# The convolution's LayerNorm chain in a two-layer encoder kernel: a raised priority, buffers of its own, one PSUM bank

## The chip, the cores and the metric

The kernel runs on one core of one Trainium2 chip. The metric is the device time of one execution in microseconds (us), the median of several runs. A profiled execution, taken apart from these runs, gives the trace: the instructions of PE (TensorE matmuls; PEld is its weight load), DVE (VectorE), ACT (ScalarE), POOL (GpSimd) and the queue of SP (SyncE), which issues most DMAs.

## The reference

Two layers work on x, 512 tokens of 1024 features in float32. Each adds half a SwiGLU feed-forward network, then a mixer, then half a second feed-forward network, and ends in an RMS norm. The mixer projects the normed x once and has two parts: attention with 8 heads, and a convolution module. The change lies in the convolution's LayerNorm:

```python
def layer_norm(x, g, b):
    mu = jnp.mean(xf, axis=-1, keepdims=True)
    xc = xf - mu
    y = xc * lax.rsqrt(jnp.mean(xc * xc, axis=-1, keepdims=True) + EPS)
    return (y * g + b)

def conv_group(u_raw, conv_w, conv_b, ln_g, ln_b):
    a, g = u_raw[..., :CONV_W], u_raw[..., CONV_W:]
    u = a * jax.nn.sigmoid(g)
    y = lax.conv_general_dilated(u, conv_w, ...)      # causal, depthwise, 31 taps
    return jax.nn.silu(layer_norm(y + conv_b, ln_g, ln_b))

x = x + jnp.concatenate([attn, conv], axis=-1) @ w_out[l]
```

## The kernel before

**Layout.** Features lie on the 128 partitions and tokens along the free axis, so a 512-wide convolution output is four tiles `ys[0..3]` of 128 x 512. A sum over features is a sum over partitions; the kernel makes it on PE with a matrix of ones. A float32 product is made of three PE products of high and low parts (`mm3`, L157 to L160: high x high, high x low, low x high). `split` (L163) makes the parts: ACT casts the high one (L165), DVE subtracts for the low one (L166).

**The order of the work.** The program names tiles and dependences; a planner lays the instructions of each engine in one order when the program is built, by priority (the order in which the lines are traced, unless it is changed) and by when it holds inputs and buffers to be free. On the chip each engine takes its instructions in that order and waits at the first one that isn't ready. `tc.issue_after(i)` places what is traced under it behind instruction i on its engine. `tmp()` (L98) hands out one of 5 temporaries, `bank()` (L101) one of 7 PSUM banks; the eighth PSUM bank, tag `cv`, holds the accumulator of convolution tiles 0 and 3.

**The mixer.** After the projections (L816), a loop over steps (L929) runs the eight heads in stages: `turn` (L833), `scores` (L846, with the maximum on DVE L861 and Exp on ACT L865), `turn_p` (L870, transposes L880 and copies L883), `values` (L886, L895 to L905), and `turn_out` (L908), which splits the output of each pair of heads into `at[0..3]`. The convolution's taps are traced after it (L941): for tiles 0 and 3 on DVE (L953) with ACT's copy out of PSUM at the end (L961), for tile 1 on ACT (L957) and POOL (L959), for tile 2 on PE (L659), ACT and POOL. They fill engines beside attention.

**The chain after the taps (L973 to L998)**, the place of the change:

- `early_groups` (L967): the output projection's first four blocks begin with their attention half, k = 0 to 3, twelve products each, behind the last head's scores. They are placed by hand in four parts: the first ahead of the chain, the second after the mean (L982), the third after the token factor (L988), the fourth after the spread (L990).
- the mean: POOL adds tiles 0, 1 and 2 into a temporary (L975, L976), DVE adds tile 3 (L977), PE spreads the mean over all partitions (L979) into a bank.
- ACT's table for Silu is loaded early by a one-element Silu (L981).
- DVE subtracts the mean from each tile (L985). ACT squares each (L188 into a ring slot, L191 into temporaries), DVE adds the squares (L195).
- `token` (L207): eight one-column matmuls sum the squares (L202), DVE scales (L209), POOL raises to -1/2 (L177).
- `spread` (L214): DVE makes a diagonal in a temporary (L217), PE multiplies it by ones (L221), so that 1/rms stands on all partitions in a bank.
- DVE multiplies each tile by it into a temporary z (L995), ACT applies gain, bias and Silu into another (L997), and `split` makes `cv`.

Then the projection's first four blocks get their convolution half (L1004, k = 4 to 7), and after them blocks 4 to 7 all eight k. Their weights take the buffers that the first four release; POOL makes their low parts (L148). x is updated at L1010, and the second feed-forward network follows.

Of the kernel before, what the change touches and what calls it, by code (L numbers as in the profile page):

```python
# [7 lines left out]
FP = mybir.dt.float32  # L8
# [3 lines left out]
AF = mybir.ActivationFunctionType  # L12
ALU = mybir.AluOpType
AX = mybir.AxisListType

P = 128
D = 1024
S = 512
# [3 lines left out]
H = 8  # L22
# [6 lines left out]
CW = 512  # L29
CK = 31  # L30
F = 2816
NF = F // P
EPS = 1e-6
# [16 lines left out]
QFOLD = 0  # L50
# [1 line left out]
EARLY = "s"  # L52
PRELOAD = 1
E1 = 1
E2 = 2
E3 = 3
WOG = 4
WAKE = 10
KS = (0, 2, 4, 6, 1, 3, 5, 7)
WOP = 4  # L60
# [18 lines left out]
def encoder_kernel(ctx: ExitStack, tc: tile.TileContext, xT, consts, vecs, rgain, wgu1, wd1, wdq1,  # L79
# [8 lines left out]
    psum = ctx.enter_context(tc.tile_pool(name="psum", bufs=7, space=PSUM))  # L88
    uid = [0]

    def nm(s):
        uid[0] += 1
        return f"{s}{uid[0]}"

    def slot(dt=FP, w=S):
        return ring.tile([P, w], dt, tag="r", name=nm("r"))

    def tmp(w=S, dt=FP):  # L98
        return tmps.tile([P, w], dt, tag="t", name=nm("t"))

    def bank():  # L101
        return psum.tile([P, S], FP, tag="ps", name=nm("ps"))

    def tiny(tag, w, dt=FP):
        return small.tile([P, w], dt, tag=tag, name=nm(tag))

    V, A, G, T = nc.vector, nc.scalar, nc.gpsimd, nc.tensor
# [17 lines left out]
    onesm = cpool.tile([P, P], FP, name="onesm")  # L125
# [8 lines left out]
    def vv(l, name):  # L134
        o, w = VOFF[name]
        return vec[:, l, o:o + w]
# [42 lines left out]
    class Stats:  # L179
# [2 lines left out]
        def __init__(self):  # L182
            self.acc = self.tail = None

        def add(self, src, scale=1.0, last=False, eng=None, apart=False):
            if self.acc is None:
                self.acc = slot()
                A.activation(self.acc, src, AF.Square, scale=scale)  # L188
                return
            sq = tmp()  # L190
            A.activation(sq, src, AF.Square, scale=scale)  # L191
            if apart:
                self.tail = sq
                return
            (eng or (V if last else G)).tensor_tensor(self.acc, self.acc, sq, ALU.add)  # L195

        def sums(self):
            ps = bank()
            parts = [self.acc] + ([self.tail] if self.tail is not None else [])
            for part in parts:  # L200
                for t in range(NT):
                    order["sums"] = T.matmul(ps[:, t:t + 1], part[:, t * P:(t + 1) * P], ones[:, 0:1],  # L202
                                             start=part is self.acc and (t == 0 or len(parts) == 1),
                                             stop=part is parts[-1], skip_group_check=len(parts) > 1).ins
            return ps[:, 0:NT]

        def token(self, n):  # L207
            self.ve = small.tile([P, NT], FP, tag="vtok", name=nm("vtok"), bufs=4)
            V.tensor_scalar(self.ve, self.sums(), 1.0 / n, EPS, ALU.mult, ALU.add)  # L209
            r = small.tile([P, NT], FP, tag="rtok", name=nm("rtok"), bufs=4)  # L210
            rsqrt(r, self.ve)
            return r

    def spread(r):  # L214

        dg = tmp()
        V.tensor_tensor(dg.rearrange("p (t j) -> p t j", t=NT),  # L217
                        ident[:, None, :].to_broadcast([P, NT, P]),
                        r[:, :, None].to_broadcast([P, NT, P]), ALU.mult)
        ps = bank()  # L220
        order["spread"] = T.matmul(ps, ones, dg, start=True, stop=True).ins  # L221
        return ps

# [397 lines left out]
    def mix_body(kpool, l, gx, norm, done):  # L621
        u, order = [], {}
        diag = kpool.tile([P, PT, Q], FP, tag="m", name=nm("m"), bufs=11)
# [6 lines left out]
        ys = [kpool.tile([P, S], FP, tag=f"y{c}", name=nm("y"), bufs=1) if n else None for c, n in enumerate(TAPS)]  # L630
# [40 lines left out]
        cqT, ckT, pq, scqs, vs = [], [], [], [], []  # L671
# [159 lines left out]
        heads = [{} for _ in range(H)]  # L831
# [14 lines left out]
        def scores(h):  # L846
            qT, kT = heads[h]["qk"]
            b01, b2, b3 = bank(), bank(), bank()
            if h % 2 == 0:
                heads[h]["sums"] = small.tile([P, NT, 2], FP, tag="sums", name=nm("sums"), bufs=3)  # L850
            sums = heads[h - h % 2]["sums"]
            mx = small.tile([P, NT], FP, tag="mx", name=nm("mx"), bufs=3)
            pi = []
            ps = [slot() for _ in range(3)]
            ps = [ps[0][:, 0:128], ps[0][:, 128:384], ps[1][:, 0:384], ps[2]]
            for i in range(NT):
                n = (i + 1) * P
                o = (b01[:, 0:128], b01[:, 128:384], b2[:, 0:384], b3)[i]
                T.matmul(o, qT[0:DQ, i * P:(i + 1) * P], kT[0:DQ, 0:n], start=True, stop=False)  # L859
                heads[h]["s"] = T.matmul(o[:, n - 64:n], mrow, mneg, start=False, stop=True).ins  # L860
                V.tensor_reduce(mx[:, i:i + 1], o, axis=AX.X, op=ALU.max, negate=True)  # L861
                p = ps[i]
                if QFOLD:
                    V.tensor_tensor(mx[:, i:i + 1], mx[:, i:i + 1], scqs[i][:, h:h + 1], ALU.mult)
                A.activation(p, o, AF.Exp, bias=mx[:, i:i + 1], scale=scqs[i][:, h:h + 1] if QFOLD else 1.0,  # L865
                             accum_out=sums[:, i, h % 2:h % 2 + 1])
                pi.append(p)
            heads[h]["p"] = pi

# [51 lines left out]
        with tc.issue_after(order["turned"]):  # L921
            for t in range(NT):
                ps = up_kv(wv, t)
# [5 lines left out]
        for step in range(H + 6):  # L929
            if step == PSTEP:  # L930
                conv_pe()
            for stage, lag in STAGES:
                h = step - lag
# [6 lines left out]
        cw, cb = vv(l, "cw"), vv(l, "cb")  # L940
        for c, n in enumerate(TAPS):  # L941
            tap = lambda k: cw[:, c * CK + k:c * CK + k + 1]
            acc = psum.tile([P, S], FP, tag="cv", name=nm("cv"), bufs=1) if n < CK else None
            if n and c != PC:
                A.activation(ys[c], u[c], AF.Identity, scale=tap(CK - 1), bias=cb[:, c:c + 1])
            for s in range(n, CK):
                k = CK - 1 - s
                if s == 0:
                    A.activation(acc, u[c], AF.Identity, scale=tap(k), bias=cb[:, c:c + 1])  # L949
                elif s == n:  # L950
                    A.activation(acc[:, s:], u[c][:, :S - s], AF.Copy, scale=tap(k))
                else:
                    V.scalar_tensor_tensor(acc[:, s:], u[c][:, :S - s], tap(k), acc[:, s:], ALU.mult, ALU.add)  # L953
            for s in range(PT if c == PC else 1, n):
                k = CK - 1 - s
                pr = kpool.tile([P, S], FP, tag="pr", name=nm("pr"), bufs=4)
                A.activation(pr[:, s:], u[c][:, :S - s], AF.Copy, scale=tap(k))  # L957
                with tc.issue_after(order["keys"]) if s >= PAUSE or c > 1 else nullcontext():
                    order["conv"] = G.tensor_tensor(ys[c][:, s:], ys[c][:, s:], pr[:, s:], ALU.add).ins  # L959
            if not n:  # L960
                A.copy(u[c], acc)  # L961
                ys[c] = u[c]
            elif n < CK:
                V.tensor_tensor(ys[c][:, n:], ys[c][:, n:], acc[:, n:], ALU.add)
        early = []

        def early_groups(ms):  # L967
            with tc.issue_after(heads[H - 1][EARLY]):
                for m in ms:
                    early.append(bank())  # L970
                    group(early[m], wo[m], at, range(4), KD)

        early_groups(range(E1))  # L973
        ysum = tmp()
        G.tensor_tensor(ysum, ys[0], ys[1], ALU.add)  # L975
        G.tensor_tensor(ysum, ysum, ys[2], ALU.add)  # L976
        V.tensor_tensor(ysum, ysum, ys[3], ALU.add)  # L977
        pm = bank()
        T.matmul(pm, onesm, ysum, start=True, stop=True)  # L979
        if PRELOAD:  # L980
            A.activation(tiny("pre", 1), ysum[:, 0:1], AF.Silu)  # L981
        early_groups(range(E1, E2))  # L982
        st = Stats()
        for c in range(4):
            V.tensor_tensor(ys[c], ys[c], pm, ALU.subtract)  # L985
            st.add(ys[c], eng=V)
        r = st.token(CW)
        early_groups(range(E2, E3))  # L988
        pr = spread(r)
        early_groups(range(E3, WOG))  # L990
        lg, lb = vv(l, "lg"), vv(l, "lb")
        cv = []
        for c in range(4):
            z = tmp()
            V.tensor_tensor(z, ys[c], pr, ALU.mult)  # L995
            s = tmp()
            A.activation(s, z, AF.Silu, bias=lb[:, c:c + 1], scale=lg[:, c:c + 1])  # L997
            cv.append(split(s))  # L998

        ac = at + cv  # L1000
        for m0 in range(0, KD, WOG):
            ms = range(m0, min(m0 + WOG, KD))
            os = [bank() for _ in ms] if m0 else early
# [78 lines left out]
    st = Stats()  # L1082
# [192 lines left out]
```

## Time and profile before

| | us |
|---|---|
| median of 3 runs (lowest to highest) | 1806.21 (1804.67 to 1807.08) |
| the profiled execution's own time | 1806.27 |
| its span, first to last instruction | 1804.5 |
| PE busy | 1785.5 |
| DVE busy | 1497.7 |
| ACT busy | 1095.8 |
| POOL busy | 382.7 |

Read it from PE, which is busy in nearly all of the span. An instruction of PE is counted with a modelled end, so consecutive products overlap in the rows; the distance from one start to the next is what one costs. The mean granted clock of PE is 0.998 of full speed. Feed-forward networks take most of the time; the two mixers are the places where POOL works, and layer 0's convolution norm lies at about 497 to 525 us, layer 1's 894 us later.

### The profile page before, as it was taken

To read this page: it belongs to the slowest core of one execution; us is meant where nothing else is said; L and a number is where in the kernel's file an instruction comes from. 1 tells how busy PE (TensorE), PEld (TensorE's weight loads), DVE (VectorE), ACT (ScalarE), POOL (GpSimd) and SP (SyncE) were. 2 spreads that over 40 slices of the span, in tenths; PEclk is the share of its full clock that TensorE was granted. 3 is DMA by queue.
4 is the path that set the end of the run, shared out by engine and by line. 5 is a ranking of instruction groups with operands and counts; after the bars stand their busy time and mean duration, and the time that the engine had idled before them with its cause. 6 is when DMAs were issued, how large, how long until landed. Compare 5 with 4: busy or idle time off the path is not lost.

```text
span 1804.5 us, 29201 instructions
## 1 busy us (share of the span) xinstructions
PE 1785.5 (99%) x11302; PEld 1584.6 (88%) x11302; DVE 1497.7 (83%) x2309; ACT 1095.8 (61%) x1699; POOL 382.7 (21%) x313
## 2 busy tenths in 40 slices
PE   9999999999999999999999999999999999999998
PEld 7899999888668899999888999998976688999997
DVE  7898988689945989898779989876998559989883
ACT  5675756467843575756645757554777435757564
POOL 1000000258623000000310000002685310000002
PEclk9999999999999999999999999999999999999999
DMA  5657574325103466665426575743260126575742
GB/s 170 164 137 187 128 187 111 107 88 135 53 14 110 122 160 158 158 159 134 123 65 169 124 193 123 193 109 115 75 170 7 36 87 158 144 177 139 181 118 73
DMA packets 71946, 228.26 MB, mean 126 GB/s; under 512 B 8448, under 2 KB 9600, under 8 KB 71808
## 3 DMA queue, kind: packets, MB, share of 16 engines
q1 hardware_dynamic: 55536, 171.87, 30.0%
q0 software_dynamic: 16128, 54.53, 17.6%
q8 instruction: 88, 1.44, 0.3%
q14 instruction: 50, 0.41, 0.1%
q10 hardware_dynamic: 144, 0.00, 0.0%
HBM read 222.19 MB, written 2.10 MB: 124 GB/s over the span
## 4 chain that ended last, share of the span: by engine, by line
PE 56%; DVE 3%; ACT 1%; POOL 0%; issue 0%; ACTq 0%; DVEq 0%; POOLq 0%
PE ps L158 14%; PE ps L160 14%; PE ps L159 14%; PE ps L377 7%; PE ps L378 4%; DVE cv L953 1%; PE ps L902 0%; PE ps L859 0%; DVE mx L861 0%; DVE wl L250 0%; PE ps L202 0%; POOL sck L177 0%; PE ps L880 0%; PE ps L221 0%; DVE kn L810 0%
## 5 line engine op out<-in xcount | busy, mean ns | idle before, releaser
L158 PE MATMUL ps<-r,wh 128*128 128x256 f32 (+1 forms) x2556 | 810.7, 321 | 4.1 <-ACT r L165 1.4
L159 PE MATMUL ps<-r,wh 128*128 128x256 f32 (+1 forms) x2556 | 813.7, 319 | 0.5 <-DVE r L166 0.5
L160 PE MATMUL ps<-r,wl 128*128 128x256 f32 (+1 forms) x2364 | 756.3, 322 | 0.2 <-DVE wl L250 0.2
L158 PEld LDWEIGHTS ps<-r,wh 128*128 128x128 f32 x2556 | 484.1, 189 | 50.5 <-ACT wh L142 3.6
L159 PEld LDWEIGHTS ps<-r,wh 128*128 128x128 f32 x2556 | 485.0, 190 | 37.4 <-DVE r L166 2.6
L160 PEld LDWEIGHTS ps<-r,wl 128*128 128x128 f32 x2364 | 448.6, 190 | 34.8 <-DVE wl L148 0.7
L377 PE MATMUL ps<-xj,wh 128*128 128x512 f32 x864 | 303.8, 391 | 0.0
L142 ACT CAST wh<-raw 128x1024 fp32r<-128x1024 f32 (+3 forms) x148 | 132.4, 901 | 209.6 <-PE ps L159 126.5
L248 ACT CAST wh<-fr 128x1024 fp32r<-128x1024 f32 (+1 forms) x160 | 157.7, 986 | 106.2 <-DVE fr L414 42.3
L394 POOL DMA_DIRECT2D ls<-in_wgu x72 | 62.7, 870 | 734.7 <-ACT ls L393 524.4
L148 DVE TENSOR_TENSOR wl<-raw,wh 128x1024 fp32r<-128x1024 f32 (+3 forms) x132 | 144.6, 1103 | 88.0 <-ACT wh L142 87.4
L250 DVE TENSOR_TENSOR wl<-fr,wh 128x1024 fp32r<-128x1024 f32 (+1 forms) x160 | 182.1, 1138 | 20.5 <-ACT wh L248 20.4
L377 PEld LDWEIGHTS ps<-xj,wh 128*128 128x128 f32 x864 | 161.4, 188 | 30.1
L378 PE MATMUL ps<-xj,ls 128*128 128x256 f32 x576 | 161.3, 280 | 0.0
L959 POOL TENSOR_TENSOR y<-y,pr 128x495 f32<-128x495 f32 (+29 forms) x90 | 120.8, 1343 | 46.6 <-ACT pr L957 41.0
L248 ACT CAST wh<-raw 128x1024 fp32r<-128x1024 f32 (+1 forms) x100 | 98.2, 982 | 45.4 <-PE ps L159 24.6
L250 DVE TENSOR_TENSOR wl<-raw,wh 128x1024 fp32r<-128x1024 f32 (+1 forms) x100 | 113.4, 1134 | 14.2 <-ACT wh L248 13.8
L378 PEld LDWEIGHTS ps<-xj,ls 128*128 128x128 f32 x576 | 108.3, 188 | 0.0
L393 ACT ACTIVATE ls<-fr 128x1024 fp32r<-128x1024 f32 (+1 forms) x56 | 56.1, 1002 | 75.0 <-PE ps L378 42.8
L195 POOL TENSOR_TENSOR r<-r,t 128x512 f32<-128x512 f32 x45 | 74.1, 1656 | 128.8 <-ACT t L191 128.2
L953 DVE SCALAR_TENSOR_TENSOR cv<-m,vec,cv 128x511 f32<-128x511 f32 (+14 forms) x120 | 87.8, 732 | 3.7 <-ACT cv L949 2.2
L394 POOL DMA_DIRECT2D ls<-in_wdq x32 | 27.7, 865 | 262.2 <-ACT ls L393 262.2
(245 smaller groups left out, 2930.8 us busy)
## 6 DMA issues: line engine op xcount, KB each, us to landing
fr<-in_wgu SPq DMA_DIRECT2D x112, 512.0 KB, 4.2
ls<-in_wgu POOLq DMA_DIRECT2D x72, 512.0 KB, 6.3
raw<-in_wgu SPq DMA_DIRECT2D x62, 512.0 KB, 4.5
fr<-in_wdq SPq DMA_DIRECT2D x48, 384.0 KB, 4.7
ls<-in_wdq POOLq DMA_DIRECT2D x32, 384.0 KB, 4.7
raw<-in_wd SPq DMA_DIRECT2D x32, 384.0 KB, 3.1
raw<-in_wd SPq DMA_DIRECT2D x32, 256.0 KB, 2.7
raw<-in_wcv SPq DMA_DIRECT2D x16, 512.0 KB, 3.5
```

What stands on the lines that cost most here:

```text
L142: order["cast"] = A.copy(hi[:, :w], raw[:, :w]).ins
L148: (G if kind in POOLW.split() else V).tensor_tensor(lo[:, :w], raw[:, :w], hi[:, :w].bitcast(FP), ALU.subtract)
L158: T.matmul(o, lh, rh, start=first, stop=False, skip_group_check=free)
L159: T.matmul(o, lh, rl, start=False, stop=False, skip_group_check=free)
L160: order["mm"] = T.matmul(o, ll, rh, start=False, stop=last, skip_group_check=free).ins
L248: A.copy(hi[:, :w], src[:, :w])
L250: order["lo"] = V.tensor_tensor(lo[:, :w], src[:, :w], hi[:, :w].bitcast(FP), ALU.subtract).ins
L377: T.matmul(o, w[0][:, c], both, start=start and k == 0, stop=False, skip_group_check=True)
L378: last = T.matmul(o[:, 0:HS], w[1][:, c], both[:, 0:HS], start=False, stop=k == 3, skip_group_check=True).ins
L394: G.dma_start(out=lo[:, :n], in_=w, accum_op=ALU.add)
L953: V.scalar_tensor_tensor(acc[:, s:], u[c][:, :S - s], tap(k), acc[:, s:], ALU.mult, ALU.add)
L959: order["conv"] = G.tensor_tensor(ys[c][:, s:], ys[c][:, s:], pr[:, s:], ALU.add).ins
```

## The change

The links from the sum of the four tiles to the spread of 1/rms are traced under a raised priority (400 places). Their buffers are tiles that the convolution has done with: the sum, the second and fourth square and the diagonal lie in `u[1]`, the first square, into which the others are added, in `u[2]`, the third in `diag`. The three matmul steps write to the bank with tag `cv`. The early groups 1 to 3 are traced together after the chain. z and the Silu's output are written in place into the tiles `ys`. The table's preload and the Silus are placed behind the last head's Exps, which `scores` now notes.

```diff
-E2 = 2
-E3 = 3
 WOG = 4
+CHAIN = 400
...
+    def behind(ins):
+        stack = ExitStack()
+        for i in ins:
+            stack.enter_context(tc.issue_after(i))
+        return stack
+
+    def conv_bank():
+        return psum.tile([P, S], FP, tag="cv", name=nm("cv"), bufs=1)
...
-        def add(self, src, scale=1.0, last=False, eng=None, apart=False):
+        def add(self, src, scale=1.0, last=False, eng=None, apart=False, into=None):
             if self.acc is None:
-                self.acc = slot()
+                self.acc = slot() if into is None else into
                 A.activation(self.acc, src, AF.Square, scale=scale)
                 return
-            sq = tmp()
+            sq = tmp() if into is None else into
...
-    def spread(r):
+    def spread(r, made=bank, dg=None):
-        dg = tmp()
+        dg = tmp() if dg is None else dg
...
-        ps = bank()
+        ps = made()
...
         early_groups(range(E1))
-        ysum = tmp()
-        G.tensor_tensor(ysum, ys[0], ys[1], ALU.add)
-        G.tensor_tensor(ysum, ysum, ys[2], ALU.add)
-        V.tensor_tensor(ysum, ysum, ys[3], ALU.add)
-        pm = bank()
-        T.matmul(pm, onesm, ysum, start=True, stop=True)
+        st = Stats()
+        with tc.high_priority(CHAIN):
+            ysum = u[1]
+            G.tensor_tensor(ysum, ys[0], ys[1], ALU.add)
+            G.tensor_tensor(ysum, ysum, ys[2], ALU.add)
+            V.tensor_tensor(ysum, ysum, ys[3], ALU.add)
+            pm = conv_bank()
+            T.matmul(pm, onesm, ysum, start=True, stop=True)
+            for c in range(4):
+                V.tensor_tensor(ys[c], ys[c], pm, ALU.subtract)
+                st.add(ys[c], eng=V, into=(u[2], u[1], diag.rearrange("p a b -> p (a b)"), u[1])[c])
+            r = st.token(CW, conv_bank)
+            pr = spread(r, conv_bank, u[1])
         if PRELOAD:
-            A.activation(tiny("pre", 1), ysum[:, 0:1], AF.Silu)
-        early_groups(range(E1, E2))
-        st = Stats()
-        for c in range(4):
-            V.tensor_tensor(ys[c], ys[c], pm, ALU.subtract)
-            st.add(ys[c], eng=V)
-        r = st.token(CW)
-        early_groups(range(E2, E3))
-        pr = spread(r)
-        early_groups(range(E3, WOG))
+            with behind(heads[H - 1]["exps"]):
+                A.activation(tiny("pre", 1), ysum[:, 0:1], AF.Silu)
+        early_groups(range(E1, WOG))
...
-            z = tmp()
-            V.tensor_tensor(z, ys[c], pr, ALU.mult)
-            s = tmp()
-            A.activation(s, z, AF.Silu, bias=lb[:, c:c + 1], scale=lg[:, c:c + 1])
+            z = s = ys[c]
+            V.tensor_tensor(z, z, pr, ALU.mult)
+            with behind(heads[H - 1]["exps"]):
+                A.activation(s, z, AF.Silu, bias=lb[:, c:c + 1], scale=lg[:, c:c + 1])
```

More of the change, by code (lines that the diff above doesn't have):

```diff
@@ L195, in add, with sums @@
             (eng or (V if last else G)).tensor_tensor(self.acc, self.acc, sq, ALU.add)
-        def sums(self):
-            ps = bank()
+        def sums(self, made=bank):
+            ps = made()
             parts = [self.acc] + ([self.tail] if self.tail is not None else [])
@@ L205, in sums, with token @@
             return ps[:, 0:NT]
-        def token(self, n):
+        def token(self, n, made=bank):
             self.ve = small.tile([P, NT], FP, tag="vtok", name=nm("vtok"), bufs=4)
-            V.tensor_scalar(self.ve, self.sums(), 1.0 / n, EPS, ALU.mult, ALU.add)
+            V.tensor_scalar(self.ve, self.sums(made), 1.0 / n, EPS, ALU.mult, ALU.add)
             r = small.tile([P, NT], FP, tag="rtok", name=nm("rtok"), bufs=4)
@@ L219, in spread @@
                         r[:, :, None].to_broadcast([P, NT, P]), ALU.mult)
-        ps = bank()
+        ps = made()
         order["spread"] = T.matmul(ps, ones, dg, start=True, stop=True).ins
@@ L864, in scores @@
                     V.tensor_tensor(mx[:, i:i + 1], mx[:, i:i + 1], scqs[i][:, h:h + 1], ALU.mult)
-                A.activation(p, o, AF.Exp, bias=mx[:, i:i + 1], scale=scqs[i][:, h:h + 1] if QFOLD else 1.0,
-                             accum_out=sums[:, i, h % 2:h % 2 + 1])
+                heads[h].setdefault("exps", []).append(A.activation(p, o, AF.Exp, bias=mx[:, i:i + 1], scale=scqs[i][:, h:h + 1] if QFOLD else 1.0,
+                             accum_out=sums[:, i, h % 2:h % 2 + 1]).ins)
                 pi.append(p)
@@ L942, in mix_body @@
             tap = lambda k: cw[:, c * CK + k:c * CK + k + 1]
-            acc = psum.tile([P, S], FP, tag="cv", name=nm("cv"), bufs=1) if n < CK else None
+            acc = conv_bank() if n < CK else None
             if n and c != PC:
```

## The prediction

> **What bounds the kernel now.** I read the page first, then the engines' busy time in stretches around the end of the mixer, then PE's waits, and last the timeline there, engine by engine.
>
> ```profile
> span 1804.5 us, 29201 instructions
> PE 1785.5 (99%) x11302; PEld 1584.6 (88%) x11302; DVE 1497.7 (83%) x2309; ACT 1095.8 (61%) x1699; POOL 382.7 (21%) x313
> ```
>
> PE is busy for 99% of the span, so only three things can change the time: PE idling, PE at a lower clock, or PE doing other work. The edit leaves PE's products as they are. So the question is what PE loses near the changed lines. The stretch view of layer 0 shows it (columns: stretch, its length, busy time and count of each engine, then the granted clock), with the slow stretch of layer 1 last:
>
> ```profile
> 485.00:495.00 10.00, 10.00 (x72) 6.38 (x71) 9.85 (x20) 6.24 (x19) 0.00 (x0) 1.00 0.01 2
> 495.00:502.70 7.70, 7.70 (x73) 5.22 (x71) 4.95 (x11) 4.68 (x11) 2.54 (x2) 1.00 0.01 2
> 502.70:510.00 7.30, 6.47 (x28) 3.68 (x28) 1.98 (x3) 2.10 (x3) 0.00 (x0) 1.00 0.00 0
> 513.50:516.70 3.20, 1.10 (x8) 1.13 (x9) 1.74 (x3) 0.48 (x1) 0.00 (x0) 0.92 0.00 0
> 516.70:519.50 2.80, 2.80 (x8) 2.22 (x9) 0.85 (x2) 0.00 (x0) 1.03 (x1) 0.50 0.00 0
> 525.00:535.00 10.00, 10.00 (x45) 8.23 (x46) 3.77 (x6) 4.18 (x7) 0.29 (x1) 1.00 0.01 2
> ...
> 1410.60:1413.60 3.00, 3.00 (x8) 2.33 (x9) 0.85 (x2) 0.00 (x0) 1.03 (x1) 0.50 0.00 0
> ```
>
> PE is dense up to 502.7 us and again from 525. Between them it idles, most of all from 513.5 to 516.7, and then runs at half its clock for 2.8 us. DVE paces the stretch to 495 (9.85 of 10.00) and has room after it: 2.75 us free to 502.7, 5.32 us to 510. The timeline of that place, rows of all engines in order of start (start, length, engine, line, what, idle before it and who ended it):
>
> ```profile
> 493.32 0.59 ACT L961 COPY m<-cv 128x512 f32<-128x512 f32 x1 [0.17 <-DVE cv L953]
> 497.16 1.28 POOL L975 TENSOR_TENSOR t<-m,y 128x512 f32<-128x512 f32 x1 [15.60 <-DVE r L166]
> 498.52 1.27 POOL L976 TENSOR_TENSOR t<-t,y 128x512 f32<-128x512 f32 x1
> 506.83 0.69 DVE L905 TENSOR_TENSOR t<-ps,t 128x512 f32<-128x512 f32 x1 [4.22 <-PE ps L902]
> 508.19 1.28 ACT L981 ACT_TABLE_LOAD   x1
> 508.20 0.69 DVE L166 TENSOR_TENSOR r<-t,r 128x512 fp32r<-128x512 f32 x1 [0.68 <-ACT r L165]
> 508.23 0.50 PE L158 MATMUL ps<-r,wh 128*128 128x512 f32 x1 [0.61 <-ACT r L165]
> 508.81 0.68 DVE L977 TENSOR_TENSOR t<-t,m 128x512 f32<-128x512 f32 x1
> 508.95 0.50 PE L159 MATMUL ps<-r,wh 128*128 128x512 f32 x1 [0.22 <-DVE r L166]
> 509.64 1.10 PE L979 MATMUL ps<-t,onesm 128*128 128x512 f32 x2
> 510.78 0.69 DVE L985 TENSOR_TENSOR m<-m,ps 128x512 f32<-128x512 f32 x1 [1.28 <-PE ps L979]
> 513.17 2.28 DVE L195 TENSOR_TENSOR r<-r,t 128x512 f32<-128x512 f32 x3
> 515.60 1.29 PE L202 MATMUL ps<-ones,r 128*128 128x1 f32 x8 [2.10 <-DVE r L195]
> 516.93 0.16 DVE L209 TENSOR_SCALAR vtok<-ps 128x4 f32<-128x4 f32 x1 [1.47 <-PE ps L202]
> 517.17 1.03 POOL L177 TENSOR_TENSOR rtok<-vtok,minus_half 128x4 f32<-128x4 f32 x1 [17.38 <-DVE vtok L209]
> 518.24 0.69 DVE L217 TENSOR_TENSOR t<-cst,rtok 128x512 f32<-128x512 f32 x1 [1.15 <-POOL rtok L177]
> 520.91 1.02 PE L221 MATMUL ps<-t,ones 128*128 128x512 f32 x2
> 521.97 0.69 DVE L995 TENSOR_TENSOR t<-m,ps 128x512 f32<-128x512 f32 x1 [3.04 <-PE ps L221]
> ```
>
> The chain of the convolution's norm runs from L977 at 508.81 to the first use of the spread at 521.97: 13.16 us, in which PE meets it three times (L979, L202, L221). It starts late for two reasons that the rows show: POOL's first add sat 15.60 us because its temporary was still read by L166, and L977, whose inputs were there at 498.52 + 1.27 = 499.79, stood on DVE behind attention's L905 (idle 4.22 us) and L166.
>
> **The change, part by part.** *Buffers of its own* end the 15.60 us: the two adds can go as soon as POOL is done with the taps. *The priority* lets L977 go as soon as its last input, L961's copy, is there at 493.32 + 0.59 = 493.91. So the chain can begin some 15 us earlier and, at its 13.2 us, end near 507. PE's own work then sets the end. What goes from PE's time, in both layers:
>
> ```profile
> PE ps L202 <- DVE r L195: 4.2, 2, 2.1
> ...
> 516.75 0.77 PE L158 MATMUL ps<-m,wh 128*128 128x512 f32 x1
> 519.76 0.40 PE L159 MATMUL ps<-r,wh 128*128 128x512 f32 x1
> 520.00 0.39 PE L160 MATMUL ps<-r,wl 128*128 128x512 f32 x1
> 1410.46 0.76 PE L158 MATMUL ps<-m,wh 128*128 128x512 f32 x1
> 1413.96 0.39 PE L160 MATMUL ps<-r,wl 128*128 128x512 f32 x1
> 524.30 0.39 PE L160 MATMUL ps<-r,wl 128*128 128x512 f32 x1
> 524.83 1.20 PE L158 MATMUL ps<-r,wh 128*128 128x512 f32 x4
> ```
>
> - A, the wait at the squares' sums (from the waits: total, times, longest): 4.2 us.
> - B, the half clock after it. At full clock products start 0.23 us apart (519.76 to 520.00, and the bulk of the stage). In layer 0 seven products took 519.76 - 516.75 = 3.01 us for 7 x 0.23 = 1.61: 1.40 lost. In layer 1 eight took 3.50 for 1.84: 1.66 lost. Together 3.1 us.
> - C, the wait of the first early group for the last head's split: 0.61 + 0.22 = 0.83 us in layer 0, taken twice 1.7 us. It goes if the other three groups, no longer placed by hand behind links of the chain, fill it: k = 0 and 1 of four groups are 24 products, 5.5 us.
>
> A + B + C = 9.0 us. PE is dense behind this place (10.00 of 10.00 from 525), so what is won here is kept.
>
> What it costs. *POOL's add beside a DVE that sets the pace*: it moves from 498.52, where DVE had room, to the end of the taps.
>
> ```profile
> 475.17 6.39 POOL L959 TENSOR_TENSOR y<-y,pr 128x486 f32<-128x486 f32 x5
> 482.05 0.68 DVE L166 TENSOR_TENSOR m<-t,m 128x512 fp32r<-128x512 f32 x1
> ...
> 1438.42 2.85 POOL L148 TENSOR_TENSOR wl<-raw,wh 128x1024 fp32r<-128x1024 f32 x1
> 1439.53 2.82 DVE L148 TENSOR_TENSOR wl<-raw,wh 128x1024 fp32r<-128x1024 f32 x1
> 1448.01 1.23 DVE L148 TENSOR_TENSOR wl<-raw,wh 128x1024 fp32r<-128x1024 f32 x1 [0.22 <-ACT wh L142]
> ```
>
> POOL ends the taps at 481.56; L976 would run to about 482.84. DVE's L166, with two operands in SBUF, starts at 482.05. The pair at 1438 shows what happens: DVE's subtraction, 1.23 us by itself, took 2.82 beside POOL's, ending 1.1 us after POOL's end. So L166 waits 482.84 - 482.05 = 0.8 us, 1.6 us for two layers, in a stretch where DVE paces attention. Bounds: nothing, if L976 falls elsewhere or PE covers it, and 1.27 each, a whole add. I take 0.8. [...]
>
> *The chain in front of attention on DVE.* Its DVE work is 0.68 (L977), 2.39 (L985, 510.78 to 513.17), 2.28, 0.16 and 0.69: 6.2 us, out of 2.75 + 5.32 us free to 510, where L977 is counted as busy already. Attention's last split may come some 3 us later than 508.89. That is covered: it feeds only k = 3 of four groups, 12 products, 2.8 us, and PE's early groups would end near 524.83 less layer 0's A, B and C (2.1 + 1.4 + 0.83), 520.5. It is covered until 520.5 - 2.8 = 517.7, over 8 us late; if the cover is gone, each us later is a us lost. Cost 0.
>
> *Waits added.* Three matmul steps in the one convolution bank, which acc's copy must leave first: pm waits for L961 anyway, the sums for the subtractions, the spread for L209; 0. The shared u[1]: the fourth square waits for the add that reads the second, the diagonal for the last add, both the chain's own order; at most one add, 0.7 us, of a chain with 10 us to spare (from spread to first product takes 524.83 - 521.97 = 2.9 us, so a chain that ends at 507 is ready at 510 for a need at 520.5); 0. The table's preload now reads u[1] after the diagonal: behind it in ACT's order stand the Silus and splits, and the 1.28 us load fits beside the spread (1.02) and L995 (0.69); 0, up to 1.3. Silus behind the last Exp: it runs before 497, 0. In-place z and s: 8 temporaries fewer, 0. No DMA is added or moved by itself, and SP's queue is as it was.
>
> *PE's order* is unknown: an order made at compile time can put the sums too early again. Per layer that is between 0 and A + B, 3.65 us; I take 0, by the nearest row, PE 7.70 of 7.70 busy with attention where the sums would now fall (495 to 502.7).
>
> Sum: 9.0 - 1.6 = 7.4 us won. The profiled execution took 1806.27 us (span 1804.5), 0.06 from the median 1806.21: **1798.9 us**.
>
> **The rivals.** *All of it*: L976 slips between two taps, L166 doesn't wait, and the switch to the convolution's products (524.30 + 0.23 to 524.83, 0.30 us) closes too: 9.0 + 0.6 = 9.6, 1796.7 us. For: POOL was free for 15 us. Against: DVE is full at 482. Smaller gaps between PE's stages could bring 2 or 3 us more, 1794.
>
> *The wait only moves*: PE, in order, stands at the sums in their new place as long as before, and the clock halves again. A and B stay, C's 1.7 is eaten by the 1.6: 1806.2 us. A priority that does nothing would give the same time. For: in the rows above PE came to the sums 2.1 us early with products ready behind them, so the order held at compile time was that wrong. Against: attention's short matmuls, not products, now stand between. [...]
>
> *Slower: attention is locked behind the chain on DVE.* If the order interleaves so that attention's last copies and L905 stand behind each link and its gaps (1.28, 1.47, 1.15, 3.04 us), the last split moves by the whole 13.2 us, to 522.1. Then k = 3 of four groups (2.8 us) ends at 524.9, today's time; beyond that point each us counts. With the table load (1.28) and L166 (0.8) in the same path, and a clock halved after the pause (12 products, 2.8 us more at 0.46), it is 4.9 us a layer: 1816 us; from 1.8 us a layer on it can be seen. For: DVE does sit idle in front of the chain's links today with others behind. Against: 8 us of room.
>
> **How the numbers follow.** Forecast 1798.9: 0.5. All of it: 0.2. The wait only moves: 0.17. Slower: 0.13. About 0.2%, 3.6 us, is what a measurement of this kernel can tell from no change. Faster by more is all of the first two but a few hundredths, with those parts of the third where half remains: 0.7; same 0.17; slower 0.13. The range reaches from 1794 to 1806.5, which leaves out the slower case and little else.
>
> **What would show it.** Right: in layer 0 L975 near 481, L977 near 494, PE's L202 with no wait over 1 us, no stretch at clock 0.50, the first convolution product near 520 instead of 524.83, and L166 near 482 at about 1.5 us. Wrong: a wait of 2 us at L202 in attention's tail, PE waiting for L165 or L166 of the last split after all other early products are done, a second table load between Exps, or time lost in stages that the diff doesn't touch.

## The result and the profile after

The changed kernel takes 1798.15 us (median of 5 runs, 1797.97 to 1799.34) against 1806.12 (5 runs, 1804.55 to 1807.08): 8.0 us less, a ratio of 0.9959 with a 95% interval of 0.9945 to 0.9974. The profiled execution took 1799.34 us. Line numbers are 8 higher than before, those of the chain's own lines some 10 (L202 is now L210, L221 is L229, L158 is L166, L166 is L174, L859 is L867; L975 is L985).

The page after, its span and its busy time:

```profile
span 1796.6 us, 29187 instructions
PE 1780.5 (99%) x11302; PEld 1582.9 (88%) x11302; DVE 1502.8 (84%) x2309; ACT 1093.6 (61%) x1699; POOL 382.7 (21%) x313
```

PE issues the same 11302 matmuls in a span 7.9 us shorter. PE's waits after (what waited for what: total us, times, longest):

```profile
PE ps L166 <- ACT r L173: 2.0, 2, 1.0
PE ps L867 <- ACT r L873: 1.7, 3, 0.7
...
PE ps L867 <- DVE r L891: 0.8, 2, 0.4
```

The 4.2 us at the squares' sums head the list no more; they are not on it at all. In their place stand smaller waits: the convolution's products for a split (2.0 us), and attention's scores for Exps and copies (1.7 and 0.8 us). The stretches of layer 0 after (length, busy time and count of PE, PEld, DVE, ACT and POOL, granted clock, and the DMA's share and GB/s):

```profile
504.41:521.21 16.80, 15.78 (x74) 11.47 (x73) 5.81 (x11) 4.19 (x7) 1.03 (x1) 1.00 0.00 0
502.70:510.00 7.30, 7.30 (x45) 4.72 (x43) 2.88 (x6) 1.69 (x4) 0.00 (x0) 1.00 0.00 0
...
513.50:516.70 3.20, 3.20 (x16) 2.61 (x15) 0.34 (x1) 1.30 (x2) 0.00 (x0) 1.00 0.00 0
516.70:519.50 2.80, 2.80 (x12) 1.99 (x11) 1.10 (x2) 0.37 (x1) 0.00 (x0) 1.00 0.00 0
519.50:525.00 5.50, 4.48 (x21) 3.35 (x20) 3.95 (x7) 4.63 (x8) 0.00 (x0) 1.00 0.00 0
```

From 502.7 to 510, where PE was busy 6.47 of 7.30 us, it is full now. From 513.5 to 519.5 PE is full too and its clock 1.00, where before it was busy 1.10 of 3.20 us and then ran at 0.50. All of the idle time left is the 1.02 us in the last row. The first line spans the work from the first early product to the first convolution product. The timeline after, with the rows that answer to the prediction's:

```profile
463.49 1.27 POOL L985 TENSOR_TENSOR m<-m,y 128x512 f32<-128x512 f32 x1
464.73 18.14 POOL L967 TENSOR_TENSOR y<-y,pr 128x495 f32<-128x495 f32 x14
482.32 1.08 DVE L174 TENSOR_TENSOR m<-t,m 128x512 fp32r<-128x512 f32 x1
482.94 1.59 POOL L986 TENSOR_TENSOR m<-m,y 128x512 f32<-128x512 f32 x1
484.88 0.49 PE L867 MATMUL ps<-r,r 96*128 96x128 f32 x2 [0.64 <-ACT r L873]
494.54 0.69 DVE L987 TENSOR_TENSOR m<-m,m 128x512 f32<-128x512 f32 x1
496.43 1.10 PE L989 MATMUL cv<-m,onesm 128*128 128x512 f32 x2
504.89 0.68 DVE L203 TENSOR_TENSOR m<-m,m 128x512 f32<-128x512 f32 x1
510.15 1.05 PE L210 MATMUL cv<-ones,m 128*128 128x1 f32 x8
512.54 0.69 DVE L225 TENSOR_TENSOR m<-cst,rtok 128x512 f32<-128x512 f32 x1 [0.18 <-POOL rtok L185]
513.31 1.28 ACT L997 ACT_TABLE_LOAD   x1 [0.30 <-DVE m L225]
517.35 1.02 PE L229 MATMUL cv<-m,ones 128*128 128x512 f32 x2
521.21 1.20 PE L166 MATMUL ps<-r,wh 128*128 128x512 f32 x4 [1.02 <-ACT r L173]
1411.28 1.20 PE L166 MATMUL ps<-r,wh 128*128 128x512 f32 x4 [1.01 <-ACT r L173]
```

Read it from the top. POOL's first add slips between two taps, and its second goes as soon as the taps are done. One matmul of the scores, at 484.88, waits 0.64 us for an Exp. DVE's last add (L987) runs at 494.54 and not at 508.81. The squares are added at 505.57, 4.6 us before PE comes to their sums at 510.15. The diagonal is ready at 513.23, but PE comes to the spread (L229) only at 517.35, 4.1 us late, and that lateness reaches the first convolution product as a wait of 1.02 us. That product starts at 521.21 and not at 524.83.

### The profile page after: what moved, and what is told of

Its sections match the earlier page's. It is cut to its first block, busy times and chain, and to the rows that moved or that the text cites. A ratio compares the mean times of both kernels' runs of the same rounds, so it can differ in the third digit from the quotient of the medians.

```text
span 1796.6 us, 29187 instructions
## 1 busy us (share of the span) xinstructions
PE 1780.5 (99%) x11302; PEld 1582.9 (88%) x11302; DVE 1502.8 (84%) x2309; ACT 1093.6 (61%) x1699; POOL 382.7 (21%) x313
## 4 chain that ended last, share of the span: by engine, by line
PE 56%; DVE 3%; ACT 1%; POOL 0%; issue 0%; ACTq 0%; DVEq 0%
PE ps L166 14%; PE ps L168 14%; PE ps L167 14%; PE ps L385 7%; PE ps L386 4%; DVE cv L961 0%; PE ps L910 0%; PE ps L867 0%; DVE mx L869 0%; DVE wl L258 0%; POOL sck L185 0%; PE ps L888 0%; PE ps L210 0%; DVE kn L818 0%; PE ps L672 0%
## 5 line engine op out<-in xcount | busy, mean ns | idle before, releaser
L166 PE MATMUL ps<-r,wh 128*128 128x256 f32 (+1 forms) x2556 | 809.6, 320 | 4.7 <-ACT r L173 2.0
L166 PEld LDWEIGHTS ps<-r,wh 128*128 128x128 f32 x2556 | 483.6, 189 | 50.0 <-ACT wh L150 4.0
L492 DVE SCALAR_TENSOR_TENSOR x<-ps,x 128x512 f32<-128x512 f32 x112 | 76.7, 685 | 8.1 <-PE ps L168 7.6
```

Of the source, the lines that this page charges most:

```text
L166: T.matmul(o, lh, rh, start=first, stop=False, skip_group_check=free)
L492: return V.scalar_tensor_tensor(v, o.rearrange("p (m t) -> p m t", m=2), 0.5 * sign, v, ALU.mult, ALU.add).ins
```

## The experiments

The prediction gave each part of the change a share: the buffers free POOL's adds, and the priority lets DVE's last add (L977) go early. The first experiments take these apart. Theory 1 has the buffers carry the gain. Theory 2 has the priority carry it, so that the buffers alone would leave the order and the time as they were. The later experiments ask where the gain that is still missing goes. Line numbers in e1, e5 and e9 are near those of the kernel before, in e4 some two higher; in e2, e3 and e8 they are those of the changed kernel, in e6, e7 and e10 one higher.

| kernel | edit | median us | ratio to before (95%) |
|---|---|---|---|
| changed | | 1798.15 | 0.9959 (0.9945 to 0.9974) |
| e1 | before, the sum in `u[1]` | 1805.64 | 1.0001 (0.9993 to 1.0010) |
| e5 | e1, the preload behind the Exps | 1797.29 | 0.9949 (0.9937 to 0.9962) |
| e2 | changed, no priority | 1802.74 | 0.9986 (0.9977 to 0.9994) |
| e3 | changed, old buffers | 1820.65 | 1.0081 (1.0068 to 1.0094) |
| e8 | changed, old banks | 1805.80 | 0.9997 (0.9988 to 1.0005) |
| e4 | before, the pause filled | 1803.05 | 0.9984 (0.9976 to 0.9993) |
| e6 | changed, the spread earlier on PE | 1796.20 | 0.9943 (0.9930 to 0.9955) |
| e7 | e6, second add on DVE | 1798.32 | 0.9956 (0.9943 to 0.9970) |
| e9 | e5, the sum on DVE | 1795.93 | 0.9943 (0.9930 to 0.9955) |
| e10 | e6, the sum on DVE | 1795.27 | 0.9938 (0.9925 to 0.9952) |

### e1: the sum's buffer alone

```diff
-        ysum = tmp()
+        ysum = u[1]
```

> The kernel before with one line changed: the sum of the four tiles lies in u[1] instead of a temporary. No priority, no other buffer, the hand-placed early groups kept. Theory 1 (what kept the chain late was the temporary that POOL waited 15.6 us for): the links move up by themselves, in the program's order 15 more products now stand between the mean and the sums, so the 2.1 us wait and the half clock behind it go: 7.3 us less, about 1799 us. Theory 2 (what kept it late was DVE's order, and only the priority mends that): 1806 us, wait at the sums still 2 us.

It took 1805.64 us: no gain, as theory 2 had it, but for a reason of its own. The chain did move up and the sums' wait and the half clock were gone. The timeline of e1 shows what took their place:

```profile
495.38 1.28 ACT L981 ACT_TABLE_LOAD   x1
496.89 1.28 ACT L865 ACT_TABLE_LOAD   x1
499.02 0.44 PE L880 MATMUL ps<-cst,r 128*128 128x128 f32 x2 [1.97 <-ACT r L865]
520.47 1.28 ACT L997 ACT_TABLE_LOAD   x1 [7.96 <-DVE t L995]
523.85 1.19 PE L158 MATMUL ps<-r,wh 128*128 128x512 f32 x4 [1.42 <-ACT r L165]
```

The one-element Silu reads the sum. With the sum ready early, it stands on ACT between the last head's Exps: a load for Silu, a load back for Exp, and a third for the real Silus. PE waits 1.97 us for an Exp and 1.42 us for a split, in each layer. These waits are 6.7 us in the two layers, most of the gain that e5 then shows: it was there and was spent on table loads.

### e5: the sum's buffer, with the preload behind the Exps

```diff
-        ysum = tmp()
+        ysum = u[1]
...
-            A.activation(tiny("pre", 1), ysum[:, 0:1], AF.Silu)
+            with ExitStack() as stack:
+                for i in heads[H - 1]["exps"]:
+                    stack.enter_context(tc.issue_after(i))
+                A.activation(tiny("pre", 1), ysum[:, 0:1], AF.Silu)
```

> The kernel before with two parts of the change alone: the sum of the tiles in u[1], and the table's preload behind the last head's Exps. No priority, no other buffer, early groups placed by hand. Theory 1 (the sum's buffer is what made the chain late; alone it lost its gain because the preload slipped between the Exps): against the 1805.6 us of the sum's buffer alone the waits of 2.0 us at the last transposes and 1.4 us at the first Silu go, twice: 1798.9 us. Theory 2 (the priority and the other buffers carry a good part): not below 1802 us.

It took 1797.29 us (1796.42 to 1798.53), the whole gain of the change and not to be told from it. It has no priority, no other new buffer, the common banks, and the early groups placed by hand as before. Its PE waits, and three rows of its timeline:

```profile
PE ps L859 <- ACT r L865: 1.8, 3, 0.7
...
PE ps L859 <- DVE r L883: 0.8, 2, 0.4
```

```profile
482.06 1.11 DVE L166 TENSOR_TENSOR m<-t,m 128x512 fp32r<-128x512 f32 x1
494.31 0.69 DVE L977 TENSOR_TENSOR m<-m,m 128x512 f32<-128x512 f32 x1
512.48 1.02 PE L202 MATMUL ps<-ones,r 128*128 128x1 f32 x8
```

PE waits neither at the sums nor at the first convolution product, and attention's scores lose what they lose in the changed kernel. DVE's last add goes at 494.31 in place of 508.81, with no priority raised. So the buffer for which POOL stood 15.60 us before L975 was the cause, of DVE's late add too, and theory 1 holds in its core: one buffer carries the gain, once ACT's table is kept out of its way. The preload's new place was not run by itself; in the kernel before, the load at 508.19 already comes after the last Exp, which ended at 496.89, so it had nothing to win there.

### e2: the change without the priority

```diff
-        with tc.high_priority(CHAIN):
+        with nullcontext():
```

> The changed kernel without its raised priority, all else kept. Theory 1 (the buffers do it): the mean's matmul keeps its early place; only the spread stands 8 products later in PE's order (behind all 48 instead of 40), which adds 8 x 0.23 = 1.8 us to the wait at the first convolution product in each layer: about 1801.8 us. Theory 2 (the priority does it): about 1806 us, the chain begins late again.

1802.74 us (12 runs, 1800.62 to 1808.62), 4.6 more than with it. The mean keeps its early place, at 496.50, and DVE's last add too, at 494.62. The spread falls further behind in PE's order, behind all 48 early products instead of 40, and the timeline of e2 has

```profile
519.02 1.02 PE L229 MATMUL cv<-m,ones 128*128 128x512 f32 x2
522.88 1.19 PE L166 MATMUL ps<-r,wh 128*128 128x512 f32 x4 [2.84 <-ACT r L173]
```

The first convolution product waits 2.84 us in place of 1.02, so 3.6 us more in two layers. The traced execution was the fastest of the twelve, with a span only 2.2 us longer than the changed kernel's; the rest of the 4.6 us stays open. What the rows show of the priority is the later place of the spread (and of the sums, 1.1 us); e5, where the early groups are placed by hand around the spread, does without it.

### e3: the priority and the bank, with the old buffers

```diff
-            ysum = u[1]
+            ysum = tmp()
...
-                st.add(ys[c], eng=V, into=(u[2], u[1], diag.rearrange("p a b -> p (a b)"), u[1])[c])
+                st.add(ys[c], eng=V)
...
-            pr = spread(r, conv_bank, u[1])
+            pr = spread(r, conv_bank)
```

> The changed kernel with its priority and bank, but with the sum, the squares and the diagonal in temporaries and a ring slot as before. Theory 1 (the buffers do it): the chain comes late in spite of the priority; the order has the mean behind 44 of the 48 early products, so PE meets nearly the whole chain with nothing to do, some 9 us of waits a layer and slow clock behind them: 1810 to 1820 us. Theory 2 (the priority does it): about 1799 us.

1820.65 us, 14.5 slower than before. Two rows of e3's timeline, its waits, and a stretch of it:

```profile
497.16 1.28 POOL L985 TENSOR_TENSOR t<-m,y 128x512 f32<-128x512 f32 x1 [15.59 <-DVE r L174]
515.50 1.02 PE L989 MATMUL cv<-t,onesm 128*128 128x512 f32 x2
```

```profile
PE cv L210 <- DVE r L203: 7.7, 2, 3.8
PE ps L166 <- ACT r L173: 5.7, 2, 2.8
PE cv L229 <- DVE t L225: 4.4, 2, 2.2
```

```profile
525.00:535.00 10.00, 6.82 (x16) 4.29 (x17) 5.27 (x9) 5.00 (x8) 0.00 (x0) 0.56 0.00 1
```

POOL waits its 15.59 us again: a raised priority does not start a chain whose buffer is still being read. The mean now comes at 515.50, behind 44 of the 48 early products; the last four stand between it and the sums, and nothing stands between the later links. So PE stands at each of them and the granted clock is 0.56 from 525 to 535. In the kernel before, with a chain as late, early groups placed by hand stand between the links. The 14.5 us are thus the price of the other parts of the change together, without the chain's buffers; what the priority alone would cost there was not run.

### e8: the change with the common banks

```diff
-            pm = conv_bank()
+            pm = bank()
...
-            r = st.token(CW, conv_bank)
-            pr = spread(r, conv_bank, u[1])
+            r = st.token(CW)
+            pr = spread(r, dg=u[1])
```

> The changed kernel with the chain's three matmul steps in the seven common banks again. In the order the mean stands behind the first 3 early products, the sums behind 14 more steps of about 3.7 us, the spread 2 products later. Theory (the bank matters through the order only: the mean's matmul comes 8 us later, and PE meets the links too early): waits of 1.2 us at the sums and 1.7 us at the spread a layer, the one at the first convolution product gone: about 1801.5 us, up to 1804 if the clock halves. Rival (the bank doesn't matter): 1798 us.

1805.80 us, no gain left and worse than expected. The mean falls to 503.70 on PE, 7.3 us later than in the changed kernel, and the links behind it stand too early for it. Rows and stretches of e8:

```profile
503.70 1.02 PE L989 MATMUL ps<-m,onesm 128*128 128x512 f32 x2
509.99 1.21 PE L210 MATMUL ps<-ones,m 128*128 128x1 f32 x8 [0.34 <-DVE m L203]
513.38 2.04 PE L229 MATMUL ps<-m,ones 128*128 128x512 f32 x2 [1.12 <-DVE m L225]
```

```profile
510.00:513.50 3.50, 2.38 (x11) 1.69 (x11) 1.30 (x3) 0.19 (x1) 1.03 (x1) 0.60 0.00 0
513.50:516.70 3.20, 3.20 (x6) 1.88 (x7) 1.24 (x3) 1.81 (x3) 0.00 (x0) 0.50 0.00 0
```

PE's waits here are for the links' inputs, none for a bank, so the bank seems to matter through the order. e5 uses the common banks, has its mean later still, at 504.76, and waits for no link: there 18 early products stand between mean and sums and 12 between sums and spread, here 7 and 2. Why the planner puts the mean later with the common banks was not tried.

### e4: the pause filled, to weigh the half clock by itself

```diff
+        fill = psum.tile([P, S], FP, tag="cv", name=nm("cv"), bufs=1)
+        with tc.issue_after(outer["product"]):
+            for _ in range(FILL):
+                filled = T.matmul(fill, ones, ysum, start=True, stop=True).ins
...
-        r = st.token(CW)
+        with tc.issue_after(filled):
+            r = st.token(CW)
```

This is the kernel before with two matmuls more, whose result nobody reads, in the 2.1 us for which PE waited ahead of the sums. The chain stays as late as it was.

> The kernel before, with two matmuls more (0.9 us each, into the unused convolution bank, result not used) in the 2.1 us in which PE waits ahead of the sums. The wait stays, only PE is busy in it. Theory (the half clock comes from that pause): the clock stays at 1.00 behind the sums and 3.1 us are won in the two layers: 1803 us. Rival (the slow clock has another cause, the one-column matmuls or the stage itself): clock 0.50 again and 1806 us.

1803.05 us (11 runs, 1802.36 to 1804.08): 3.1 less than before, by adding work. Timeline and stretch of e4 (each filler shows as two in the rows, so the two are x4):

```profile
513.78 1.88 PE L988 MATMUL cv<-t,ones 128*128 128x512 f32 x4
516.03 1.02 PE L204 MATMUL ps<-ones,r 128*128 128x1 f32 x8 [0.37 <-DVE r L197]
```

```profile
516.70:519.50 2.80, 2.80 (x15) 2.37 (x15) 0.86 (x2) 0.00 (x0) 1.03 (x1) 1.00 0.00 0
```

The sums start 0.4 us later than before, yet the stretch behind them runs at clock 1.00, with 15 matmuls where it had 8 at 0.50. That is B by itself, and the gain is the prediction's 3.1 us, within an interval of 1.3 to 4.3.

### e6: the spread ahead of the early groups 2 and 3

```diff
-        early_groups(range(E1, WOG))
+        early_groups(range(E1, 2))
+        with tc.issue_after(outer["spread"]):
+            early_groups(range(2, WOG))
```

> The changed kernel with early groups 2 and 3 placed behind the spread on PE. Theory (what is left over is that PE comes to the spread 4.1 us after its diagonal is ready, so the convolution's products come 1.02 us late, and 0.16 us of start-up): 24 products, 5.5 us, now stand behind the spread and cover the 2.9 us from spread to first product; the wait goes in both layers: 1795.8 us. Rival (PE, now early at the sums and the spread, waits there as before the change, and the clock may halve): 1798 to 1804 us.

1796.20 us (1795.48 to 1797.29). The first convolution product waits no longer, for the spread goes up to 514.51, as e6's timeline shows:

```profile
514.51 1.10 PE L230 MATMUL cv<-m,ones 128*128 128x512 f32 x2 [0.33 <-DVE m L226]
```

It is 1.95 us less than the changed kernel. The wait removed was 2.0 us in two layers, and the 0.33 us at the spread are new in each. The intervals of e6 and of the changed kernel overlap; their runs do not.

### e7, e9, e10: who makes the sum

Attention's scores wait 1.7 + 0.8 us for Exps and copies in the changed kernel and 0.4 before. The 0.8 us cost nothing that the rows show: in layer 0 the matmul that waits 0.38 us, at 471.40, starts 5.11 us after the scores' one at 466.29, and before the change the same two were 5.11 us apart. New is the 0.64 us at 484.88, and the collision of POOL and DVE near 482 us was the suspect. e7 moves the second add of e6 to DVE; e9 (from e5) and e10 (from e6) have DVE make all three, beginning with tile 3:

```diff
-            G.tensor_tensor(ysum, ysum, ys[2], ALU.add)
+            V.tensor_tensor(ysum, ysum, ys[2], ALU.add)
```

```diff
-        G.tensor_tensor(ysum, ys[0], ys[1], ALU.add)
-        G.tensor_tensor(ysum, ysum, ys[2], ALU.add)
-        V.tensor_tensor(ysum, ysum, ys[3], ALU.add)
+        V.tensor_tensor(ysum, ys[3], ys[0], ALU.add)
+        V.tensor_tensor(ysum, ysum, ys[1], ALU.add)
+        V.tensor_tensor(ysum, ysum, ys[2], ALU.add)
```

> As the run with the spread first, and the second add of the sum on DVE instead of POOL. Theory (POOL's add beside DVE holds L174 for 0.4 us, and with it attention's scores wait 0.64 us on PE): L174 near 482 takes 0.68 us, the wait of the scores for ACT's copy falls from 1.7 to 0.4 us, up to 1.3 us won; but only 6 products stand between sums and spread, 1.4 us for a link of 2.0 us, which gives 0.6 us a layer back: 1795.5 us. Rival (the shift has another cause, such as the earlier add between the taps): the same waits as with the spread first alone.

> The kernel with the sum's buffer and the preload behind the Exps alone, and the sum made on DVE after its last input (tile 3 first, then tiles 0, 1, 2), so that POOL has only its taps; PE's order is the same to the last row. Theory (either POOL add, by itself or by pushing the last tap's add 1.27 us back, puts a POOL add beside DVE's L166 and costs attention's scores 0.66 + 0.4 us a layer on PE): POOL ends the taps near 481.5, L166 takes 0.68 us again, those two waits go: 2.1 us less than 1797.3, 1795.2 us; DVE's two more adds (1.4 us) fall where it has room. Rival (those waits have another cause, or DVE's adds cost as much): 1797.3 us or more.

> The run with the spread first (1796.2 us), and the sum made on DVE after its last input. Theory: as above L175 takes 0.68 us and 2.1 us of waits of the scores go: 1794.1 us, the fastest of all. Rival: the mean comes 1.4 us or more later and PE, which has only 24 products ahead of the spread, waits at the sums or the spread instead: 1796 us or more.

e7 missed: 1798.32 us, and the collision is as it was. Its timeline:

```profile
464.50 18.16 POOL L968 TENSOR_TENSOR y<-y,pr 128x495 f32<-128x495 f32 x14
482.06 1.15 DVE L175 TENSOR_TENSOR m<-t,m 128x512 fp32r<-128x512 f32 x1
```

POOL's last tap, and not its second add, stands beside DVE's subtraction, which takes 1.15 us and not 0.68: the first add, at 463 us, pushes the taps back until they end at 482.66; before the change they ended at 481.56, ahead of its start at 482.05. With the sum ready later, PE also waits 0.76 us a layer at the spread, where e6 waits 0.33. With the first add gone too, the taps end at 481.95, and e9's timeline and its waits show the subtraction back at 0.68 us and most of the scores' waits gone:

```profile
482.50 0.68 DVE L166 TENSOR_TENSOR m<-t,m 128x512 fp32r<-128x512 f32 x1
```

```profile
PE ps L859 <- ACT r L865: 0.4, 1, 0.4
...
PE ps L859 <- DVE r L883: 0.2, 1, 0.2
```

That the subtraction is longer beside POOL's work, and the scores wait more with it, is shown; the price is not. e9 took 1795.93 us, 1.4 less than e5, with overlapping intervals and spans of 1794.6 and 1794.7. e10 took 1795.27 us (1795.17 to 1796.61), the lowest of all, 0.9 below e6 and not to be told from it; part of its gain goes to a spread that now waits:

```profile
513.49 1.10 PE L230 MATMUL cv<-m,ones 128*128 128x512 f32 x2 [0.70 <-DVE m L226]
```

e10 beats the kernel before by some 11 us. Against the changed kernel it is some 3 us lower, with intervals that overlap a little and runs that don't.

## Why the prediction was right, and where its terms were off

The forecast was 1798.9 us and the mechanism held: A, B and C went. Neither rival on the other side came: PE does not wait at the sums in attention's tail, and attention was not locked behind the chain on DVE. How the steps add up in layer 0 can be read from where three products start. Rows of the kernel before, a stretch and then the timeline:

```profile
502.76:524.83 22.07, 18.99 (x75) 12.90 (x74) 9.71 (x16) 6.64 (x11) 1.03 (x1) 0.92 0.00 0
```

```profile
510.81 0.40 PE L159 MATMUL ps<-m,wh 128*128 128x512 f32 x1
1418.82 1.20 PE L158 MATMUL ps<-r,wh 128*128 128x512 f32 x4 [0.16 <-ACT r L165]
```

From the first early product to the first convolution product it was 22.07 us and is 16.80: 5.27 less. PE's idle time in it falls from 22.07 - 18.99 = 3.08 to 16.80 - 15.78 = 1.02, which is 2.06. The half clock gives its 1.40. The mean's matmul now lies ahead of the stretch; before, it and one product took 510.81 - 509.64 = 1.17, so it took 0.94 without the product's 0.23. The 0.87 left lie mostly beside the waits: before the change the three starts that end a wait of 0.61, 0.22 and 2.10 come 1.01, 0.72 and 2.49 after the start ahead of them, 0.60 more than the waits and a product of 0.23 each explain. On the other side the stretch begins 504.41 - 502.76 = 1.65 later: 0.94 for the mean, and 0.71 by which attention ends later, 0.09 of it there already at 480.5, ahead of the collision. So layer 0 wins 5.27 - 1.65 = 3.62 us, and with layer 1 it is 1418.82 - 1411.28 = 7.54 at the first product there, 7.9 at the end of the span.

- **A** (4.2 us) and **C** (1.7): right, and too small. Without the new wait of 1.02 and the mean, the stretch won 5.27 - 0.94 + 1.02 = 5.35 us in layer 0, where A, B and C promised 4.33. A wait cost more than its idle row, as the three starts above show. C's cause was put wrongly: it did not need the groups to be freed from their places by hand, since e5 keeps these and C is gone there too.
- **B** (3.1 us): right in size and cause; e4 removes it alone, for 3.1 us.
- **POOL's add beside DVE** (0.8 us a layer, L166 "at about 1.5 us"): the place was wrong. L985 went at 463.49, between taps, and not near 481, and it is the last tap that meets DVE's L174, which takes 1.08 us and not 0.68: 0.40 in layer 0. What PE paid is at most the 0.71 by which attention ended later, some 0.6 of it behind 480.5, where the scores' matmul at 484.88 waits. So the term was near in what it cost. e9 ties that wait to POOL's adds. (The taps end at 464.73 + 18.14 = 482.87, and L174 at 483.40, 0.53 us later. L986, begun at 482.94 beside it, takes 1.59 us, where the same add, L976, took 1.27 before.)
- **The priority's part**: wrong. The prediction needed it for DVE's last add, to pass attention's L905 and L166. Without it the add goes at 494.62 in e2 and 494.31 in e5: the sum's buffer moved it. What the priority gave lies in PE's order (e2).
- **PE's order, costed at 0**: this step failed. The sums came late enough, as the row of 7.70 of 7.70 suggested, but the spread was put 4.1 us behind its inputs, and 1.02 us a layer were lost at the first convolution product. e6 wins them back. The prediction looked for a link placed too early and not for one too late.
- **The preload, 0 to 1.3**: 0, as its load at 513.31 shows, behind the diagonal. How much could hang on it the prediction did not see: a preload that follows the sum alone cost the whole gain in e1.

So two misses met: layer 0 won 1.0 us more from the waits than was counted, and gave back 0.71 + 1.02 = 1.73 where 0.8 was allowed. That these nearly cancel, and put 1798.15 so close to 1798.9, is luck.

## What to carry to other kernels

When an engine waits long for a temporary that another stage still reads, give it a buffer of its own before touching any priority: the sum's buffer, with the preload kept out of its way, brought the whole gain, and the same change with the chain's old buffers, priority and all, was 14.5 us slower than no change. Anything that was held back only by the late buffer will move up with it, so look at once for what it drags along, a table load between Exps above all. And when a chain gets earlier, check each of its links in PE's order from both sides: a link placed far behind its inputs (4.1 us in the changed kernel, 1.02 us a layer lost) can cost time as one placed ahead of them does (waits of 0.34 and 1.12 us in e8, and a clock of 0.50 behind them).

## What the runs showed of the hardware

- In e8 the clock fell with no wait above 0.53 us just ahead of it. In layer 0 PE was busy 0.63 of the 1.50 us from 508.5 to 510, with waits of 0.53 and 0.34 us, and then ran the eight one-column matmuls. The granted clock was 1.00 from 502.7 to 510, 0.60 from 510 to 513.5 and 0.50 to 516.7. The wait of 1.12 us came only at the spread, at 513.38; the product at 511.63, ahead of it, already took 0.63 us, where the one at 508.23 took 0.40. In the kernel before, with a wait of 2.10 us ahead of the same matmuls at 515.60, the clock was 1.00 up to 516.0, 0.70 in the next half microsecond and 0.50 from 516.5 on. In e4, where full-width matmuls stand in that pause and the one-column matmuls remain behind a wait of 0.37 us, it was 1.00 from 513.5 to 519.5. In e2, where a wait of 2.84 us stands ahead of full-width products, it was 1.00 from 519.5 to 535.
- Two matmuls of which nothing is used made the kernel 3.1 us faster (e4).
- A table load takes 1.28 us on ACT; with one Silu among the Exps PE waited 1.97 us for the Exp behind it, and 1.42 us later, behind a third load (e1).
